# One core, two transformer blocks: the instruction order taken from a simulation of the engines' pipelines

## The chip, the cores and the metric

The kernel runs on one core of a Trainium2 chip. A core has five engines with an instruction queue each: TensorE (PE, with its weight loads as a row of their own, PEld), VectorE (DVE), ScalarE (ACT), GpSimd (POOL) and SyncE (SP), which here only starts DMAs. Each engine works its queue in order; semaphores make it wait for the others. The metric is the device time of one execution in microseconds.

## The reference

Two blocks of two layers each work on 512 positions of 1024 values (the first block puts 16 learned positions ahead: 528), all in float32. Cut to what matters:

```python
# block 1, per layer
proj = rms_norm(h, g) @ w_in                       # q, k, v, xr, gate
q, k = rope(rms_norm(q, gq)), rope(rms_norm(k, gk))        # norms over 64 values of a head
a = softmax(q0 @ k0.T) - lam * softmax(q1 @ k1.T)          # differential attention, causal
o_attn = rms_norm(a @ v, g_sub) * (1 - lam_init)           # norm over 128 values
o_rec = rms_norm(rg_lru(conv(xr)) * gelu(gate), g_rec)
h = h + concat(o_attn, o_rec) @ w_out
g, u = split(rms_norm(h, g2) @ w_gu);  h = h + (silu(g) * u) @ w_down

# block 2, per layer
score = sum_h iw_h * relu(iq_h @ ik.T)             # indexer, 8 heads
keep  = top_k(score, 128)                          # per query
y_dsa = softmax(dq @ dk.T over keep) @ dv          # 6 heads
y_chk = softmax(cq @ ck.T + rel_bias over a band) @ cv     # 6 heads
x = layer_norm(alpha * x + concat(y_conv, y_dsa, y_chk) @ w_out)
x = layer_norm(alpha * x + cross_attention(x, mem))
x = layer_norm(alpha * x + relu(x @ w1) ** 2 @ w2)
```

## The kernel before

Activations lie transposed, features on the 128 partitions and positions along the free dimension. Every weight block (128 columns, 512 KB) comes by a DMA of SP into `wraw`, is rounded by ScalarE to `whi` (L90), and the rest is subtracted by VectorE into `wlo` (L92; 23 blocks on GpSimd). Each product is three matmuls (`mm3`, L96 to L98: high by high, high by low, low by high), so that these three lines make up nearly all of PE's time: 264 columns at a time in block 1, 512 in block 2. `proj` runs the eight `mm3` of a block into a PSUM bank. There are eight banks by name: three `mm` (projections), two `sc` (scores), one each of `tr` (transposes), `av` (row sums and value products) and `bc` (norm factors spread over partitions).

A norm (`rnorm`) goes round four engines: PE sums the squares with the matmuls L166 into `av`; VectorE scales the sum (L170 or L172); `rsqrt` makes the inverse root by a polynomial in twelve small instructions (L136 to L147), which for the norms of queries and keys (`rows`), of the attention's output (`attend1`) and of the recurrent branch (`recout`) run on **GpSimd**: 26 chains in the program. For the 64-wide norms ScalarE then repeats the factors (`nrep`, L179). The transposes L185 spread them into `bc`, and VectorE applies them. The weight products that wait for nothing of this can fill PE's time in between.

Block 1's `attend1` takes a tile of 128 queries: scores into `sc` (L489, the mask L492, L494), their maximum on VectorE (L495), the exponent on ScalarE (L503), the difference of the two softmaxes (L506 to L511), transposes into `tr` (L518, and L523 for the last 16 keys), a split into high and low (L121, L122), and the value product into `av`. The output product `w_out` comes in two halves: the first (`w0`) needs only the recurrent branch (`rh`, `rl`), the second (`w1`) the attention (`bh`, `bl`).

Block 2's mixer first makes the indexer's heads (L898: scores into `sc`; ScalarE's relu L900; VectorE's weighted sum L902), then per block of 128 queries sixteen rounds of VectorE's MAX8 (L913) and MATCH_REPLACE8 (L914), which mark the 128 largest scores. The attention over them (`dsa`) and over the band (`A`) shares `scores` (L851, L852), `attend` (L832 to L839) and `turn` (transposes L845). A layer norm (`Norm.finish`) sums in L730, runs `rsqrt` on VectorE and spreads in L740.

What sets the order: the program is written as a list of steps (STEPS1 for a layer's mixer of block 1, STEPS2 for block 2). The tile framework hands all instructions to a scheduler, which gives each a priority by its place in the program and then simulates the machine: whenever an engine is free in its simulation, it appends to that engine's queue the instruction of the highest priority that is ready there. How long things take in that simulation thus decides what stands ahead of what.

## Time and profile before

| | |
|---|---|
| median of 3 runs | 2938.83 us (2935.24 to 2939.16) |
| the profiled execution | 2940.24 us, span 2938.5 us |
| mean granted TensorE clock | 0.983 |
| PE busy | 2812.4 us, 96% |
| VectorE, ScalarE, GpSimd busy | 58%, 42%, 15% |

The stages of the span, by the lines that run: block 1's first mixer to about 310 us, its feed-forward to 694, the second mixer to 990, its feed-forward to about 1340; block 2's first mixer to about 1610, cross attention, feed-forward; its second mixer from about 2140 to 2410; the last layer norm ends the program. Matmuls are pipelined: the times from start to start tell PE's pace, the durations overlap.

### The profile page before, as it was taken

What the parts mean: (1) busy time and instruction counts of PE and PEld (TensorE: products, weight loads), DVE (VectorE), ACT (ScalarE), POOL (GpSimd) and SP (SyncE); (2) the same over time, 40 slices, a digit from 0 to 9 for tenths busy, and PEclk for the clock granted to TensorE, in tenths of its full rate; (3) what the DMA queues carried; (4) which work ended last, traced back from release to release, by engine and by line L of the source; (5) the groups of instructions that cost most, each with busy time, mean ns of one, the idle gap of its engine ahead of it and who ended that gap; (6) DMA issues with size and microseconds to landing.
All of it is one profiled execution on the core that took longest, in us unless ns stands there. A gap on an engine that the chain in (4) does not pass through costs nothing.

```text
span 2938.5 us, 43082 instructions
## 1 busy us (share of the span) xinstructions
PE 2812.4 (96%) x16556; PEld 2451.3 (83%) x16556; DVE 1700.9 (58%) x3250; ACT 1242.1 (42%) x2218; POOL 446.9 (15%) x715
## 2 busy tenths in 40 slices
PE   7888999999888999999999999999999999999998
PEld 7888999998776788888788888888877898888887
DVE  7666534446766744446997555333589875643335
ACT  5654322224655422223675434322346754333323
POOL 1223000000323000001212021111322120211112
PEclk9999999999999999999999999999999999999999
DMA  4321332322322333334623323333245243223331
GB/s 138 91 70 48 101 94 86 95 87 79 81 72 66 111 94 91 98 91 116 165 74 109 114 65 94 93 97 97 83 113 162 61 129 90 71 94 95 99 94 65
DMA packets 96492, 277.19 MB, mean 94 GB/s; under 512 B 13344, under 2 KB 20000, under 8 KB 96288
## 3 DMA queue, kind: packets, MB, share of 16 engines
q1 hardware_dynamic: 96288, 274.45, 31.7%
q8 instruction: 131, 2.15, 0.3%
q14 instruction: 73, 0.60, 0.1%
HBM read 241.82 MB, written 2.10 MB: 83 GB/s over the span
## 4 chain that ended last, share of the span: by engine, by line
PE 84%; DVE 7%; POOL 3%; issue 2%; ACT 2%; DMA 0%; SPq 0%; ACTq 0%; DVEq 0%; POOLq 0%
PE mm L97 25%; PE mm L98 25%; PE mm L96 25%; PE av L96 1%; DVE wlo L92 1%; PE av L97 1%; POOL nwu L146 1%; PE av L98 1%; PE av L166 1%; PE bc L185 1%; POOL nwu L147 1%; PE bc L845 1%; PE av L730 1%; PE tr L845 1%; PE sc L96 0%
## 5 line engine op out<-in xcount | busy, mean ns | idle before, releaser
L96 PE MATMUL mm<-xh_all,whi 128*128 128x512 f32 (+2 forms) x2752 | 933.5, 341 | 16.4 <-ACT xh_all L269 9.9
L97 PE MATMUL mm<-xl_all,whi 128*128 128x512 f32 (+2 forms) x2752 | 937.6, 341 | 1.2 <-DVE xl_all L270 0.5
L98 PE MATMUL mm<-xh_all,wlo 128*128 128x512 f32 (+2 forms) x2752 | 934.5, 340 | 0.0
L90 ACT CAST whi<-wraw 128x1024 fp32r<-128x1024 f32 (+2 forms) x460 | 465.4, 1013 | 1041.3 <-PE mm L97 857.0
L92 DVE TENSOR_TENSOR wlo<-wraw,whi 128x1024 fp32r<-128x1024 f32 (+2 forms) x437 | 541.1, 1239 | 238.2 <-ACT whi L90 235.7
L96 PEld LDWEIGHTS mm<-xh_all,whi 128*128 128x128 f32 x2752 | 526.5, 192 | 70.5 <-ACT xh_all L269 10.1
L97 PEld LDWEIGHTS mm<-xl_all,whi 128*128 128x128 f32 x2752 | 527.3, 192 | 54.9 <-DVE xl_all L270 1.6
L98 PEld LDWEIGHTS mm<-xh_all,wlo 128*128 128x128 f32 x2752 | 528.4, 192 | 49.9
L1124 POOL TENSOR_TENSOR r<-r 128x512 f32<-128x512 f32 (+1 forms) x70 | 101.8, 1454 | 532.3 <-ACT r L1123 532.3
L98 PE MATMUL mm<-yh,wlo 128*128 128x264 f32 (+1 forms) x528 | 169.4, 321 | 0.0
L96 PE MATMUL mm<-yh,whi 128*128 128x264 f32 (+1 forms) x528 | 169.1, 321 | 0.0
L97 PE MATMUL mm<-yl,whi 128*128 128x264 f32 (+1 forms) x528 | 168.5, 319 | 0.0
L691 DVE TENSOR_TENSOR hall<-hall,mm 128x512 f32<-128x512 f32 (+1 forms) x82 | 46.5, 567 | 144.9 <-PE mm L98 144.9
L611 DVE TENSOR_TENSOR su<-mm,rbc 128x264 f32<-128x264 f32 (+1 forms) x66 | 34.2, 519 | 140.0 <-PE mm L98 140.0
L620 DVE TENSOR_TENSOR hall<-hall,mm 128x264 f32<-128x264 f32 (+1 forms) x72 | 37.1, 515 | 130.7 <-PE mm L98 130.7
L97 PEld LDWEIGHTS mm<-yl,whi 128*128 128x128 f32 x528 | 99.2, 188 | 8.6 <-DVE yl L122 0.6
L98 PEld LDWEIGHTS mm<-yh,wlo 128*128 128x128 f32 x528 | 99.0, 188 | 7.5
L96 PEld LDWEIGHTS mm<-yh,whi 128*128 128x128 f32 x528 | 99.2, 188 | 7.1
L606 DVE TENSOR_TENSOR sg<-mm,rbc 128x264 f32<-128x264 f32 (+1 forms) x66 | 34.0, 517 | 100.4 <-PE mm L98 100.3
L450 POOL MEMSET vh<- 128x128 f32 x8 | 1.6, 204 | 462.0 <-PE mm L98 411.9
L710 POOL TENSOR_TENSOR accq<-accq,nsq 128x512 f32<-128x512 f32 (+1 forms) x48 | 57.6, 1201 | 25.4 <-ACT nsq L708 24.0
L92 POOL TENSOR_TENSOR wlo<-wraw,whi 128x1024 fp32r<-128x1024 f32 x23 | 55.9, 2429 | 36.3 <-ACT whi L90 35.3
(690 smaller groups left out, 5481.7 us busy)
## 6 DMA issues: line engine op xcount, KB each, us to landing
wraw<-w2f SPq DMA_DIRECT2D x128, 512.0 KB, 3.7
wraw<-w1gu SPq DMA_DIRECT2D x88, 512.0 KB, 3.6
wraw<-w2in SPq DMA_DIRECT2D x44, 512.0 KB, 3.9
wraw<-w1in SPq DMA_DIRECT2D x40, 512.0 KB, 3.7
wraw<-w2mkv SPq DMA_DIRECT2D x32, 512.0 KB, 3.7
wraw<-w1dn SPq DMA_DIRECT2D x32, 448.0 KB, 3.3
wraw<-w1out SPq DMA_DIRECT2D x32, 256.0 KB, 2.6
wraw<-w1dn SPq DMA_DIRECT2D x16, 512.0 KB, 3.6
```

The lines of the kernel that those rows point to most:

```text
L90: nc.scalar.copy(hi[:, :kt], raw[:, :kt])
L92: (eng or nc.vector).tensor_sub(lo[:, :kt], raw[:, :kt], f(hi[:, :kt]))
L96: nc.tensor.matmul(ps, wh, xh, start=first, stop=False)
L97: nc.tensor.matmul(ps, wh, xl, start=False, stop=False)
L98: nc.tensor.matmul(ps, wl, xh, start=False, stop=last)
L606: nc.vector.tensor_mul(sg[:, a:b], p, r2[:, a:b])
L611: nc.vector.tensor_mul(su[:, a:b], p, r2[:, a:b])
L620: nc.vector.tensor_add(h[m][:, a:b], h[m][:, a:b], p)
L691: nc.vector.tensor_add(X(m, a, b), X(m, a, b), p)
L710: nc.gpsimd.tensor_add(self.accq[:, a:b], self.accq[:, a:b], sq[:, a:b])
L845: nc.tensor.transpose(ps[:, 128 * j:128 * j + 128], p[:, 128 * j:128 * j + 128], ident)
L1124: nc.gpsimd.tensor_mul(r[:, a:b], r[:, a:b], r[:, a:b])
```

## The change

The scheduler is asked to take its decisions from another simulation, one that follows the engines' pipelines.

```diff
-    with _tile.TileContext(nc) as tc:
+    with _tile.TileContext(nc, schedule_with_timeline_sim=True) as tc:
         both_blocks(tc, *args)
```

The instructions stay the same on every engine, with the same tiles; their order changes on all of them. Three places follow. A name like `mm_657` is one tile: `mm_657`, `mm_736` and `mm_761` are projections, a row with `x6` is six instructions.

PE at the first key's norm in layer 0 of block 1, from the row sums L166 to the transposes L185 that spread the factors, before:

```order
L97 MATMUL mm_657<-xl_all_71,whi_626 128x264
L166 MATMUL av_572<-cs_68,sq_518 88x2 x6
L98 MATMUL mm_657<-xh_all_70,wlo_628 128x264
...
L97 MATMUL mm_736<-xl_all_71,whi_730 128x264
L98 MATMUL mm_736<-xh_all_70,wlo_732 128x264
L185 MATMUL bc_598<-cs_68,nrep_596 128x88 x3
```

and now:

```order
L98 MATMUL sc_482<-xch_471,wgl_231 128x264
L166 MATMUL av_572<-cs_68,sq_518 88x2 x3
L96 MATMUL mm_657<-xh_all_70,whi_626 128x264
...
L98 MATMUL mm_761<-xh_all_70,wlo_732 128x264
L96 MATMUL mm_845<-xh_all_70,whi_839 128x264
L185 MATMUL bc_598<-cs_68,nrep_596 128x88 x3
```

Between the last L166 and L185 stood 28 matmuls of 264 columns; now there are 64, which reach into a third projection.

PE at the end of layer 0's attention (`tr_2960` are the last tile's transposes, `av_2971` its value product, `av_2989` the row sums of its norm, `bc_3013` the spread; `mm_3274` to `mm_3312` are of w_out's first half, `mm_3337` of its second), before:

```order
L98 MATMUL mm_3261<-rh3_2635,wlo_3259 128x264
L518 MATMUL tr_2960<-cs_68,p_2928 128x128 x4
L96 MATMUL mm_3274<-rh0_2567,whi_3257 128x264
...
L96 MATMUL av_2971<-ath_2897,vh_2218 128x256
L96 MATMUL mm_3274<-rh2_2499,whi_3257 128x264
...
L166 MATMUL av_2989<-one2_74,osq_2808 88x2 x6
L98 MATMUL mm_3299<-rh1_2153,wlo_3297 128x264
...
L96 MATMUL mm_3312<-rh3_2635,whi_3295 128x264
L97 MATMUL mm_3312<-rl3_2636,whi_3295 128x264
L185 MATMUL bc_3013<-cs_68,nwy_2998 128x88 x3
```

and now:

```order
L494 MATMUL sc_2947<-k2_2234,qs_1982 128x256
L518 MATMUL tr_2960<-cs_68,p_2928 128x128 x4
L96 MATMUL av_2971<-ath_2897,vh_2218 128x256
L523 MATMUL tr_2967<-cs_68,p_2928 16x128
L97 MATMUL av_2971<-atl_2898,vh_2218 128x256
...
L98 MATMUL av_2971<-ath_2897,vl_2219 128x256
L166 MATMUL av_2989<-one2_74,osq_2808 88x2 x6
L185 MATMUL bc_3013<-cs_68,nwy_2998 128x88 x3
L185 MATMUL bc_3017<-cs_68,nwy_2998 128x88 x3
L96 MATMUL mm_3337<-bh3_3023,whi_3333 128x264
```

All of w_out's first half now stands ahead of the last tile's scores; from L494 to the second half nothing stands between the steps of the chain.

PE in layer 0 of block 2, where the indexer's last heads (`sc_13571` to `sc_13596`) meet the first score pairs (`mm_14031`, `mm_14074` are projections), before:

```order
L898 MATMUL sc_13596<-ik_13086,iq_13085 128x512
L824 MATMUL bc_13774<-cs_68,rt_13745 128x128 x4
L96 MATMUL mm_14031<-xh_all_70,whi_14027 128x512
L851 MATMUL sc_13783<-dkh_13071,dq_13070 128x256
L852 MATMUL sc_13783<-dkl_13072,dq_13070 128x256
L97 MATMUL mm_14031<-xl_all_71,whi_14027 128x512
...
L851 MATMUL sc_13796<-dkh_13071,dq_13070 128x256
L852 MATMUL sc_13796<-dkl_13072,dq_13070 128x256
```

and now:

```order
L98 MATMUL mm_14074<-xh_all_70,wlo_14072 128x512
L898 MATMUL sc_13571<-ik_13086,iq_13085 128x512
L898 MATMUL sc_13576<-ik_13086,iq_13085 128x512
...
L898 MATMUL sc_13596<-ik_13086,iq_13085 128x512
L851 MATMUL sc_13783<-dkh_13071,dq_13070 128x256
L852 MATMUL sc_13783<-dkl_13072,dq_13070 128x256
L851 MATMUL sc_13796<-dkh_13071,dq_13070 128x256
L852 MATMUL sc_13796<-dkl_13072,dq_13070 128x256
...
L845 MATMUL tr_13792<-cs_68,p_13787 128x128
```

Six heads of the indexer and four score pairs now follow each other with no projection in between; the projections of `mm_14031` and `mm_14074` stand ahead of them.

## Rows read from the trace of the kernel before

**Rows 1.** The page: busy time by engine, and the chain that ended last.

```profile
PE 2812.4 (96%) x16556; PEld 2451.3 (83%) x16556; DVE 1700.9 (58%) x3250; ACT 1242.1 (42%) x2218; POOL 446.9 (15%) x715
PE 84%; DVE 7%; POOL 3%; issue 2%; ACT 2%; DMA 0%; SPq 0%; ACTq 0%; DVEq 0%; POOLq 0%
```

**Rows 2.** Windows (stretch, length; PE, PEld, DVE, ACT, POOL busy; clock; DMA): mixers, feed-forward.

```profile
22.00:310.00 288.00, 255.73 (x1952) 240.49 (x1953) 197.24 (x431) 163.31 (x327) 71.89 (x207) 0.94 0.28 78
300.00:375.00 75.00, 74.98 (x621) 74.76 (x621) 38.07 (x66) 24.52 (x31) 0.00 (x0) 1.00 0.32 99
694.00:990.00 296.00, 259.72 (x1563) 222.85 (x1564) 206.49 (x424) 166.10 (x317) 70.50 (x198) 0.94 0.28 77
```

**Rows 3.** Waits of PE (line, releaser: us in total, times, longest).

```profile
PE bc L185 <- ACT nrep L179: 31.5, 15, 3.2
PE bc L185 <- POOL nwy L147: 19.8, 10, 3.0
PE bc L740 <- DVE nwy L154: 10.9, 10, 3.7
...
PE sc L898 <- ACT p L900: 7.3, 9, 1.7
PE tr L518 <- DVE p L511: 5.5, 10, 1.1
```

**Rows 4.** Timeline (start, duration; idle time before and its releaser): first GpSimd chain.

```profile
51.60 1.10 PE L166 MATMUL av<-cs,sq 128*88 128x2 f32 x12
...
55.40 1.30 POOL L147 TENSOR_TENSOR nwu<-nwu,nwt 88x12 f32<-88x12 f32 x1
55.40 1.22 DVE L92 TENSOR_TENSOR wlo<-wraw,whi 128x1024 fp32r<-128x1024 f32 x1 [0.19 <-ACT whi L90]
...
58.33 0.21 POOL L147 TENSOR_TENSOR nwy<-nwu,nwy 88x12 f32<-88x12 f32 x1
58.58 0.83 ACT L179 COPY nrep<-nwy 88x768 f32<-88x768 f32 x1 [3.20 <-POOL nwy L147]
...
59.46 0.51 PE L185 MATMUL bc<-cs,nrep 88*128 88x88 f32 x3 [3.24 <-ACT nrep L179]
```

**Rows 5.** Timeline: the last GpSimd chain, one without L179.

```profile
952.83 0.25 PE L166 MATMUL av<-one,osq 128*128 128x2 f32 x1
...
957.67 0.32 PE L185 MATMUL bc<-cs,nwy 128*128 128x128 f32 x1 [1.84 <-POOL nwy L147]
```

**Rows 6.** Windows: PE at the first chain's end, and the stretch after it.

```profile
59.80:63.00 3.20, 3.20 (x18) 3.20 (x17) 1.61 (x4) 2.65 (x4) 0.10 (x1) 0.50 0.02 5
63.10:66.50 3.40, 3.40 (x30) 3.40 (x29) 3.40 (x4) 0.82 (x1) 1.70 (x1) 1.00 0.00 0
```

**Rows 7.** Timeline: one softmax tile of block 1, scores to transposes.

```profile
261.80 0.36 PE L494 MATMUL sc<-k,qs 128*128 128x256 f32 x1
...
262.20 0.42 DVE L495 TENSOR_REDUCE st<-sc 128x1 f32<-128x256 f32 x1
...
263.38 0.49 ACT L503 ACTIVATE p<-sc,st 128x272 f32<-128x272 f32 x1 [0.32 <-DVE st L501]
...
264.49 0.38 DVE L506 TENSOR_TENSOR st<-st 128x1 f32<-128x1 f32 x1
...
265.41 0.74 ACT L510 ACTIVATE p<-p,st 128x528 f32<-128x528 f32 x1 [1.00 <-DVE st L509]
...
266.18 1.23 DVE L511 SCALAR_TENSOR_TENSOR p<-p,st 128x528 f32<-128x528 f32 x1 [0.17 <-ACT p L510]
...
267.56 0.30 PE L518 MATMUL tr<-cs,p 128*128 128x128 f32 x1 [0.60 <-DVE p L511]
```

**Rows 8.** Windows: the top-k stretch of block 2, both layers.

```profile
1400.00:1510.00 110.00, 105.78 (x542) 84.99 (x543) 108.41 (x310) 73.11 (x165) 23.89 (x36) 1.00 0.50 136
2196.00:2310.00 114.00, 108.78 (x551) 87.12 (x550) 108.70 (x316) 72.94 (x167) 23.08 (x36) 0.99 0.48 132
```

**Rows 9.** Lines of VectorE by form (count; us busy, mean ns; idle before).

```profile
L913 DVE MAX8 m<-isc 128x8 f32<-128x512 f32 x32 | 21.9, 684 | 0.1
```

## The prediction

> **What bounds the kernel now.** I read the page first, then the busy times by stage, the waits of TensorE (PE), and then single chains in the timeline. PE is busy 96% of the span and carries 84% of the chain that ended last [rows 1]. So an order can win only what PE loses by waiting or by a low clock, and can lose what it uncovers. By stage: in the feed-forward stretch PE never waits and issues 621 matmuls of 264 columns in 75.0 us, 0.121 us each [rows 2]; no order helps there. In block 1's two mixer stretches PE is busy 255.7 of 288 us and 259.7 of 296 us, at a mean granted clock of 0.94 [rows 2]: that is where time lies. The waits say what ended PE's idle time [rows 3]: most is at L185, the transposes that spread a norm's result, 31.5 us behind ScalarE's copy L179 and 19.8 us behind GpSimd's last step L147. Everything else is small: 10.9 us for the LayerNorm's L740, 7.3 us for the indexer's L898, 5.5 us for the softmax's L518.
>
> **The change part by part.** No instruction is added or removed; each engine still runs its list in order, and only the lists differ. So I counted, for each chain that leaves PE and comes back, the PE work that stands between the two ends (its cover) at the paces of rows, and set it against the chain's time in the trace. Where the cover is shorter, PE waits for the difference.
>
> *A, the GpSimd norm chains.* The first one starts at 51.60 and its L185 starts at 59.46; L166 itself takes 1.1 us, so the chain proper is 6.7 us [rows 4]. Before, 28 matmuls stand in between (28 x 0.121 = 3.4 us) and PE waits 3.24 us [rows 4]; the new order puts 64 there, 7.7 us, and the wait is gone. The last chain runs from 952.83 to 957.67 with a wait of 1.84 us [rows 5]. There are 26 such chains (16 with L179, 4.7 to 7.3 us; 10 without, 3.75 to 4.9 us), 139 us in all. Their covers sum to 71 us before and 159 us now. Chain by chain the shortfall is 68 us before, of which rows 3 show 31.5 + 19.8 = 51 us, and 21 us after: eight chains stay short, two of them with nothing in between. I take the ratio on the measured wait plus the issue gap around it: 63 x (68 - 21) / 68 = 43, so **-42** (-36 if only the 51 us shrink, -47 if all the 68 do).
>
> What the chain's length rests on shows in its fifth GpSimd pair: L147 takes 1.30 us where the same operation takes 0.21 us later, and it starts at the instant at which DVE starts the 1.22 us subtraction L92 [rows 4]. The Trainium skill, page "SBUF — State Buffer", section "Who interferes with whom", says that a DVE instruction with two SBUF inputs contends with a GpSimd instruction that reads SBUF, that one fully blocks the other, and that the order of issue decides which; the trace agrees, 1.30 against 0.21 us. By that rule the new DVE order could lengthen the chains: an estimate with each at the length of the longest seen gives a shortfall of 32 in place of 21 us, 11 us more in the sum; I don't count it.
>
> *B, the clock in block 1.* After such a wait the clock falls: in the 3.2 us from 59.80 PE issues 18 matmuls at a granted clock of 0.50 (1.2 of 2.4 GHz), in the 3.4 us after that 30 at 1.00 [rows 6]. 5.6 against 8.8 per us: each us at half speed costs 0.36 us. A mean of 0.94 over 288 and 296 us [rows 2] is about 35 us at half speed in each, 12 to 13 us lost in each, 25 in all. Fewer long waits, fewer falls; but C makes new ones. Half: **-12** (0 to -25).
>
> *C, the softmax at phase ends.* In the middle of the phases nothing is lost. But the new order spends the projections and output weights early, and at the end of a phase none is left between a tile's last score L494 and its transposes L518. In six tiles the cover falls from 3.9 to 5.6 us to 0.3, 1.8, 0, 3.0, 2.0 and 0 us (7.1 in all). A tile's own operations add up to 0.36 + 0.42 + 0.49 + 0.38 + 0.74 + 1.23 = 3.6 us, and with the queues between them it took 267.56 - 261.80 = 5.8 us [rows 7]. So 6 x 3.6 - 7.1 = 14.5 at best and 6 x 5.8 - 7.1 = 28 at worst; **+17**, near the bare end, because the weight splits in those queues have then been done. What follows such a tile is bare too: the split of the transposed block before the value product (four times), the second transpose (five), the first output matmul (three). Twelve steps at about 0.7 us (the nearest row is ScalarE's copy of 0.83 us [rows 4]): **+8** (0 to 10). The query's DMAs stand nearer to their first score: **+4** (0 to 10). Block 1 thus gives -25.
>
> *D, the top-k stretch of block 2.* Here DVE, not PE, is full: busy 108.4 of 110 us and 108.7 of 114 us [rows 8], with 32 of the largest MAX8 at 0.684 us [rows 9] and as many replacements. PE loses little there (105.8 of 110 busy), because projections stand among the scores. The new order groups the scores and pulls the projections ahead, so PE reaches consumers of DVE earlier. Over the same 50 us of PE work, 83 us of DVE work (each instruction at its row's mean) stand ahead of what PE needs next, before 68. Counted from the first rope on, DVE falls behind by 18.6 us where it was 7.3 in the first layer, and by 18.1 where it was 5.6 in the second: +11 to +12 per layer, **+23** (0 if the top-k steps give way, +34 if the largest lag, 17 each, counts in full).
>
> *E, the rest of block 2's scores.* They stand in rows of eight on two banks; today L898 waits 7.3 us in nine pieces [rows 3], 0.8 us each. Ten more such waits: **+8** (0 to 30). *F, the closing LayerNorms*: covers go up in one half and down in the other; chains of 7 to 12 us against 5 to 18 us of cover give **+4** (-2 to 12) against today's 10.9 us [rows 3]. *G, the clock in block 2*: if D's and E's 31 us of waits bring half-speed stretches as in rows 6, some 22 us of them at 0.36: **+8** (0 to 14). The start, the feed-forward stages and the end of the program keep their order within a few matmuls and cost nothing: PE work covers them as now.
>
> Sum: -42 - 12 + 17 + 8 + 4 + 23 + 8 + 4 + 8 = +18 on the profiled execution's 2940.24 us, 2958. That run lies 1.4 us above the median of the three (2938.83), so **2957**. All low ends give -60, all high ends +102.
>
> **The rivals.** *Faster.* The chain gain stays and the DVE of the top-k stretch keeps up, because a top-k step only has to be done when its block's mask is used, and its lag (18 us) may be smaller than the PE work queued at that place. Place: the score pairs L851 and L852 of block 2. It decides from the point at which DVE's lag stays under what PE still has ahead; then D, E and G vanish: -42 - 12 + 17 + 8 + 4 + 4 = -21, and -34 with the whole of the clock's 25: 2905 to 2918, middle 2912. For it speaks that DVE is busy only 58% of the span [rows 1] and that the total DVE work is the same; against it that in that stretch it has nothing to spare [rows 8]. *No change*: the order doesn't bring what it is built for; the waits that A takes away come back as C, D and the same number of clock falls (A -42, B 0, C and its train +29, D +13): 2939. *Far slower*: the grouped chains queue as before's do (5.8 us for 3.6, up to 14 us for a tile in the middle of a phase). By those times the shortfall over every chain of the program would be 306 us where it was 153; the high ends of C to G are then the better prices: about +70, 3010.
>
> **How the numbers follow.** My forecast, a net loss of 6 to 50 us, has 0.45; faster 0.30; no change 0.15; far slower 0.10. The time is the first case's, 2957; its own range is 2945 to 2990. The range runs from the faster rival's low end to below the far slower one: 2905 to 3000, leaving out 0.1 on each side. A measurement of this kernel tells some 0.2% (6 us) from no change, so: faster 0.30, same 0.15, slower 0.55.
>
> **What would show it.** In the new profile: PE's wait at L185 behind L179 and L147 down from 51 to about 15 to 20 us (A); the mean clock of the mixer stretches at 0.96 to 0.97 (B); PE's wait at L518 up from 5.5 to over 20 us, at the end of each layer's attention (C); in the top-k stretch PE waiting for DVE or for ScalarE behind it by 10 us or more per layer, DVE still full (D). The forecast is wrong if that stretch takes its 110 us as before, or if the softmax tiles at the phase ends start their transposes without a wait.

## The result: 4.3% slower, outside the range

The changed kernel takes **3063.9 us** (median of 4 runs, 3061.13 to 3071.68) against 2938.99 us: a ratio of 1.0432, interval 1.0412 to 1.0453. Slower was the forecast's side, but 18 us were forecast and 125 came; even the "far slower" rival stood at 3010.

The page after, the lines that answer to [rows 1] (busy time by engine; the chain that ended last):

```profile
PE 2866.4 (94%) x16556; PEld 2502.1 (82%) x16556; DVE 1689.1 (55%) x3250; ACT 1244.8 (41%) x2222; POOL 449.9 (15%) x715
PE 77%; DVE 11%; ACT 4%; DMA 3%; issue 2%; POOL 1%; SPq 1%; DVEq 0%; ACTq 0%; POOLq 0%
```

The span went from 2938.5 to 3059.3 us, by 120.8. PE runs the same 16556 matmuls, but is busy 54.0 us longer (2866.4 against 2812.4): they ran slower. The other 66.8 us are idle time. The mean granted clock fell from 0.983 to 0.960; the stretches at half clock add up to 249 us in the trace after and 102 us before, and (249 - 102) x 0.36 = 53 us, an estimate with the price of a half-speed us that the prediction took from [rows 6], is as much as the longer busy time. So the loss has **two parts: 67 us of waits and 54 us of longer busy time, by this estimate nearly all of it the clock**. Stage by stage the estimate doesn't come out: in the table below the longer busy time (length less idle) is 7 us for 38 us at half clock in each of block 1's mixers, but 19 for 34 and 13 for 17 in block 2's. Part of block 2's is something else: the records count a matmul with nothing behind it for its whole duration, in place of the time to the next start, and PE stands idle 137 times in block 2 where it was 52.

Where it lies, by the starts of the last matmul of each stage (length; how much longer after; of it PE idle; half-clock time more), in us:

| stage | before | after | idle | at half clock |
|---|---|---|---|---|
| block 1, mixer of layer 0 (to the end of w_out) | 303.4 | +13.9 | +6.6 | +38 |
| block 1, mixer of layer 1 | 284.4 | +11.1 | +3.8 | +38 |
| block 2, mixer of layer 0, with the norm ahead | 245.7 | +38.6 | +19.5 | +34 |
| block 2, mixer of layer 1, with the norm ahead | 258.3 | +35.1 | +21.8 | +17 |
| the other nine stages together | 1846.7 | +22.1 | +15.1 | +20 |

What PE waits for after, beside [rows 3] (line, releaser: us in total, times, longest):

```profile
PE tr L518 <- DVE p L511: 17.7, 4, 6.0
PE sc L851 <- DVE st L832: 15.1, 25, 1.7
PE av L166 <- ACT sq L415: 14.7, 4, 5.1
PE mm L96 <- DVE hall L691: 10.2, 6, 2.9
...
PE bc L740 <- DVE nwy L154: 8.5, 5, 4.1
PE sc L898 <- ACT p L900: 8.5, 7, 2.6
PE bc L185 <- POOL nwy L147: 7.7, 2, 3.9
PE av L166 <- ACT osq L532: 6.2, 6, 1.8
...
PE bc L185 <- ACT nrep L179: 4.6, 4, 2.2
```

The GpSimd norms did what term A said: 31.5 + 19.8 us at L185 became 4.6 + 7.7. The softmax at phase ends did what term C said: L518 went from 5.5 to 17.7. New or grown are the row sums L166, 14.7 us behind ScalarE's squares L415 of the *next* query or key norm, and 6.2 behind L532, the squares of the attention's output; L96 behind L691 (none before), a projection that waits until VectorE has added an earlier one out of its bank; and L851, in 25 small pieces. The two of them that stood in the list before:

```profile
PE av L166 <- ACT sq L415: 3.2, 4, 1.1
PE sc L851 <- DVE st L832: 1.9, 2, 1.0
```

The stretches that answer to [rows 2] and [rows 8] (stretch, length; PE, PEld, DVE, ACT, POOL busy; clock; DMA):

```profile
22.00:317.00 295.00, 255.64 (x1897) 242.32 (x1896) 189.71 (x402) 162.42 (x326) 76.72 (x208) 0.88 0.26 72
707.00:1004.00 297.00, 255.17 (x1515) 224.19 (x1514) 193.55 (x402) 164.91 (x313) 75.15 (x203) 0.88 0.26 71
1430.00:1560.00 130.00, 112.31 (x502) 87.90 (x501) 106.32 (x301) 67.78 (x155) 22.27 (x36) 0.88 0.41 110
2270.00:2400.00 130.00, 112.05 (x510) 87.24 (x509) 105.40 (x301) 67.97 (x154) 22.52 (x35) 0.92 0.42 110
```

Block 1's mixers fell from a clock of 0.94 to 0.88, the top-k stretch from 1.00 and 0.99 to 0.88 and 0.92. And VectorE, full in that stretch before (108.4 of 110), has room after (106.3 of 130).

### The profile page after: what moved, and what is told of

Its sections match the earlier page's. It is cut to its first block, busy times and chain, and to the rows that moved or that the text cites. A ratio compares the mean times of both kernels' runs of the same rounds, so it can differ in the third digit from the quotient of the medians.

```text
span 3059.3 us, 43072 instructions
## 1 busy us (share of the span) xinstructions
PE 2866.4 (94%) x16556; PEld 2502.1 (82%) x16556; DVE 1689.1 (55%) x3250; ACT 1244.8 (41%) x2222; POOL 449.9 (15%) x715
## 4 chain that ended last, share of the span: by engine, by line
PE 77%; DVE 11%; ACT 4%; DMA 3%; issue 2%; POOL 1%; SPq 1%; DVEq 0%; ACTq 0%; POOLq 0%
PE mm L96 23%; PE mm L97 23%; PE mm L98 23%; DVE wlo L92 1%; PE av L97 1%; PE av L96 1%; PE av L98 1%; SPq L863 1%; DVE isc L914 1%; ACT whi L90 1%; PE av L166 1%; DMA dq<-nl 1%; DVE m L913 1%; DVE hall L720 1%; DVE p L832 1%
## 5 line engine op out<-in xcount | busy, mean ns | idle before, releaser
L96 PE MATMUL mm<-xh_all,whi 128*128 128x512 f32 (+2 forms) x2752 | 938.9, 343 | 18.2 <-ACT xh_all L269 9.9
L92 DVE TENSOR_TENSOR wlo<-wraw,whi 128x1024 fp32r<-128x1024 f32 (+2 forms) x437 | 536.2, 1228 | 250.0 <-ACT whi L90 247.4
L96 PEld LDWEIGHTS mm<-xh_all,whi 128*128 128x128 f32 x2752 | 532.0, 194 | 79.1 <-ACT xh_all L269 10.1
L97 PEld LDWEIGHTS mm<-xl_all,whi 128*128 128x128 f32 x2752 | 533.6, 194 | 62.7 <-DVE xl_all L763 5.4
L98 PEld LDWEIGHTS mm<-xh_all,wlo 128*128 128x128 f32 x2752 | 534.6, 194 | 56.1 <-DVE wlo L92 2.3
L96 PE MATMUL mm<-yh,whi 128*128 128x264 f32 (+1 forms) x528 | 168.6, 321 | 0.0
L691 DVE TENSOR_TENSOR hall<-hall,mm 128x512 f32<-128x512 f32 (+1 forms) x82 | 45.5, 567 | 153.6 <-PE mm L98 153.6
L96 PEld LDWEIGHTS mm<-yh,whi 128*128 128x128 f32 x528 | 99.0, 188 | 6.9
L92 POOL TENSOR_TENSOR wlo<-wraw,whi 128x1024 fp32r<-128x1024 f32 x23 | 55.7, 2423 | 88.7 <-ACT whi L90 88.6
L503 ACT ACTIVATE p<-sc,st 128x272 f32<-128x272 f32 (+4 forms) x88 | 45.6, 521 | 43.8 <-DVE st L495 23.5
```

The costliest lines, as they stand in the source:

```text
L92: (eng or nc.vector).tensor_sub(lo[:, :kt], raw[:, :kt], f(hi[:, :kt]))
L96: nc.tensor.matmul(ps, wh, xh, start=first, stop=False)
L97: nc.tensor.matmul(ps, wh, xl, start=False, stop=False)
L98: nc.tensor.matmul(ps, wl, xh, start=False, stop=last)
L503: nc.scalar.activation(p[:n, a:b], ps[:n, :b - a], AF.Exp, bias=mx, accum_out=st[:n, o + 3 + e:o + 4 + e])
L691: nc.vector.tensor_add(X(m, a, b), X(m, a, b), p)
```

## The experiments

The instructions of both kernels are the same under the same names, so an order can be carried from one program to the other: the program is first scheduled both ways, the queues of each engine are noted (`old`, `new`), and in a third pass dependencies without a wait hold an engine to a noted queue. What is not held, the scheduler of that run decides, in the same pass and so with the held queue before it. The code cuts of this section are shortened to the idea.

```diff
+    for queue in rule(traced):               # the queues that this kernel holds
+        for a, b in zip(queue, queue[1:]):
+            tc.add_manual_dep(by[b], a, no_sync, reason="order")
```

### Which half of the program, which engine's queue

`first_new`: `rule` gives block 1's part of all queues from `new`, block 2's from `old`; `second_new` the other way round.

> All engines take the new order in block 1 and the old one in block 2. In the trace after, block 1 ends 33 us later than before (1344.1 to 1377.5 us at the last down-projection). If the stages lose independently: 2939 + 33 = 2972 us, with the clock of both mixer stretches at 0.88. If block 1's loss were given back or made larger by what block 2's order expects of it: under 2955 or over 2990.

> The old order in block 1, the new one in block 2. Independent stages: 2939 + (121 - 33) = 3027 us, of it some 38 us in each mixer. If block 2 only suffers from what block 1 hands over: under 2990.

Measured: **2972.5** (ratio 1.0114, 1.0099 to 1.0129) and **3032.0** (1.0317, 1.0302 to 1.0333). 33 + 93 us, against 125 for both: the two halves lose independently, near the sizes of the stage table (33 and 87).

`pe_old`: the new scheduler, `rule` returns `[old["PE"]]`. `pe_new`: the old one with `[new["PE"]]`. `dve_old`: the new one with `[old["DVE"]]`.

> The scheduler decides by the pipelines' simulation, but TensorE's own order is held to that of the kernel before; the other engines' queues are free and come out of the new simulation. Theory 1 (TensorE's order is the cause: work that could fill is spent early and the chains stand bare): the loss goes, 2930 to 2960 us. Rival (the other engines' orders are the cause: on VectorE and ScalarE other work stands ahead of what TensorE waits for): 3020 us or more.

> The other half: the scheduler of before, TensorE held to the new order. Theory 1: 3030 to 3070 us. Rival: 2940 to 2970 us, since the other queues are again made by the old simulation.

> The new scheduler with VectorE's queue held to the old order; the other four queues are free. If VectorE's order is the cause: 2980 us or less. If an order only fits as a set with the others made with it (theory 2, after the two runs that held TensorE's queue): 3050 us or more, as those.

Measured: **3061.3**, **3158.2** and **3299.7** us. My theory 1 fell: with the old TensorE queue the new scheduler is as slow as with its own. But the rival is not shown either, for with the new TensorE queue the old scheduler is slower still, above both expectations. In `pe_old` PE waits for the GpSimd norms again and for more besides (its lines stand 3 further down):

```profile
PE bc L188 <- ACT nrep L182: 33.2, 13, 5.2
PE bc L188 <- POOL nwy L150: 27.0, 10, 3.9
PE bc L743 <- DVE nwy L157: 23.1, 7, 4.0
PE sc L901 <- ACT p L903: 11.4, 11, 2.2
```

These are other waits than the new order's, at other stages: block 1's mixers are 23.0 and 17.4 us longer than before, block 2's only 18.2 and 16.4. So neither TensorE's nor VectorE's queue alone carries the loss. Each hold of one queue, with the others made round it by the scheduler that did not make that queue, costs 120 to 360 us, while all queues held together (`first_new`, `second_new`) cost what the stage table says. This speaks for orders that fit as a set; a hold of one queue under its own scheduler, which would show what the hold itself costs, was not run.

### Is the new simulation worse, or were the step lists fitted to the old one?

`plain_old` and `plain_new`: STEPS1 and STEPS2 in plain order (all `r`, then key, query, value and attention head by head, gates last; block 2 likewise, with its top-k steps in the order of their blocks), old and new scheduler.

> The old scheduler with the step lists in plain order: in block 1 all recurrent parts first, then head by head key, query, value, attention, and the gates at the end; in block 2 projections, indexer, then dsa, then the bands. It is the base for the next kernel; 20 to 150 us over 2939, since less matrix work is left to lie beside the chains.

> The new scheduler with the same plain lists. Theory 3 (the lists of the kernel are fitted to the orders that the old scheduler makes of them, the new simulation as such is no worse): within 40 us of the plain lists with the old scheduler, on either side. Theory 4 (the new simulation makes worse orders of any list): 80 us or more over it.

Measured: **3176.8** and **3260.5** us. The base is 238 us over the kernel before, more than the 150 expected. With lists that nobody fitted, the new scheduler is 84 us slower, against 125 with the kernel's own: theory 4, at its edge. So the fit of the lists is not needed for the new simulation to lose; how much of the 125 is the fit one other list can't settle.

### Terms A and B alone

`covered`: the old scheduler, TensorE's old queue, in which 24 of the 26 spreads L185 are moved back past other matrix work.

```diff
+    for sums, spread in CHAINS:              # L166s and L185s of a GpSimd norm
+        later(spread, 7.5, q.index(sums[-1]))    # us of matrix work in between
+    return [q]
```

> Terms A and B alone: the old scheduler and TensorE's old order, in which only the spreads L185 of 24 of the 26 GpSimd norms are moved back, past other matrix work, until about 7.5 us of it stand ahead of them (where enough is there); the two norms of the recurrent branch stay. If the forecast's sizes for A and B hold: the wait at L185 behind L179 and L147 falls from 51 to under 20 us, the clock of block 1's mixers rises, 2880 to 2905 us. Rival (what is moved ahead is missing later, and the softmax tiles or the following norms stand bare, as in the new order): 2930 us or more.

Measured: **3002.3** us (1.0216, 1.0200 to 1.0233). The rival: the following norms do stand, though not for want of cover. PE's waits there (its lines stand 5 to 11 further down; L172 is the row sums, L426 the squares, L194 the spread, L428 the product that empties `bc`):

```profile
PE av L172 <- ACT sq L426: 44.4, 10, 5.8
PE sc L500 <- ACT p L514: 13.7, 11, 2.6
PE bc L194 <- DVE raw L428: 12.4, 8, 4.1
PE bc L194 <- POOL nwy L152: 11.2, 7, 3.5
```

Of the norms' waits 11.2 us are left of 51, and 44.4 us came back at the next norm's row sums (3.2 before), 13.7 at the scores L500. Why, the trace after shows at its longest L166 wait (timeline; start, duration):

```profile
162.50 0.45 PE L185 MATMUL bc<-cs,nrep 88*128 88x88 f32 x3 [0.82 <-DVE raw L417]
163.64 0.48 DVE L417 SCALAR_TENSOR_TENSOR raw<-raw,par,bc 128x264 f32<-128x264 f32 x1
166.03 0.71 DVE L420 TENSOR_TENSOR sq<-sq,ct 128x528 f32<-128x528 f32 x1
168.03 0.69 DVE L421 TENSOR_TENSOR raw<-raw,sq 128x528 f32<-128x528 f32 x1
168.75 0.63 ACT L121 CAST nh<-raw 128x528 fp32r<-128x528 f32 x1 [1.58 <-DVE raw L421]
169.29 0.64 ACT L415 ACTIVATE sq<-raw 128x528 f32<-128x528 f32 x1
169.98 0.31 PE L166 MATMUL av<-cs,sq 128*88 128x2 f32 x1 [5.11 <-ACT sq L415]
```

The tile `sq` has one buffer and two lives in `rows`: it holds the squares (L415), and after the norm the rotated half of the rope (L418 to L421). The next norm's squares need it back. So a spread that comes later makes the next L166 later. The trace alone doesn't prove it: ScalarE's queue has the key's split L121, which waits for L421 too, ahead of the squares. `apart_old`, `covered_apart` and `apart_new` give the squares another buffer, which stands in the layer anyway:

```diff
+    ss = small.tile([128, T], F32, name="ss_sq", bufs=2)
-    nc.scalar.activation(sq[:, a0:b0], raw[:, a0:b0], AF.Square)
+    nc.scalar.activation(ss[:, a0:b0], raw[:, a0:b0], AF.Square)
```

> The old scheduler and the old lists; in the norms of queries and keys the squares go to a buffer of their own (one of two that stand in the layer already), so that the next norm's squares need not wait until the rope has let go of the buffer. In the old order nothing waits there: 2930 to 2950 us. Base for the next kernel.

> The kernel with the spreads L185 moved back, whose TensorE waited 44 us for the squares L415 in place of the norms, with the squares in a buffer of their own as in the run before. If that one buffer is what gave the gain of terms A and B back: the wait at L166 for L415 falls under 10 us, 2900 to 2930 us. Rival (the next thing in line, the softmax tiles and the score banks behind the later keys, takes it): 2960 us or more.

> The new scheduler with the squares of the query and key norms in a buffer of their own (under the old one that changed nothing, 2939 us). If the one buffer, for which TensorE waits 14.7 us at L166 in the trace after, is a cause of block 1's loss: block 1 is 15 us or more shorter with the clock it gives back, 3035 to 3050 us. Rival (it is only the wait that ends last there): 3055 us or more.

Measured: `apart_old` **2939.2** us (0.9998, 0.9989 to 1.0008): nothing under the old order, as expected. `covered_apart` **2954.6**, between its two expectations: 48 us of `covered`'s loss of 64 are gone and L166's wait is 8.3 us, but it is still not faster than before. Its longest wait is now at the one bank `bc`, whose second half waits 15.0 us until VectorE has emptied the first; whether that is what keeps it from gaining was not tested. `apart_new` **3028.7** us, 35 us faster than the change as made and below the range expected. Its first mixer beside the window of block 1 above, and its wait at the softmax's transposes (two lines further down there):

```profile
22.00:300.00 278.00, 250.04 (x1925) 237.74 (x1925) 191.03 (x408) 160.38 (x325) 84.01 (x208) 0.90 0.28 78
```

```profile
PE tr L520 <- DVE p L513: 4.3, 2, 4.1
```

By stages block 1's mixers are now 6.8 and 8.6 us *shorter* than before, where they were 13.9 and 11.1 longer. But the new scheduler made other orders with that buffer: the wait at the transposes fell too, from 17.7 to 4.3 us, with no change to what the softmax works on. So the buffer, and the order that the scheduler makes with it, turned block 1's loss into a gain; what the buffer brings with the order of the change kept was not run.

`mix1_new` draws the conclusion: the squares apart, `rule` gives the new scheduler's order for this kernel in block 1's two mixers alone, the old everywhere else.

> The new order in block 1's two mixers alone, with the squares in a buffer of their own, where it made them 7 and 9 us shorter than the old; the old order everywhere else. If terms A and B hold as soon as that buffer is out of the way, and the stages are independent: 2939 - 16 = 2923 us, the lowest of all. Rival (the gain is given back at the stage's end, where the old order takes over): 2935 us or more.

Measured: **2924.2** us (0.9945, 0.9933 to 0.9958), the forecast of its expectation to 1 us, and **faster than both kernels**. The window that answers to the first of [rows 2]:

```profile
22.00:310.00 288.00, 262.17 (x2032) 249.88 (x2031) 198.49 (x425) 165.44 (x332) 84.39 (x208) 0.92 0.29 80
```

The clock there is 0.92, *lower* than the 0.94 before. Over the whole program PE stands idle 10 us less than before (115.9 against 126.0 us), and yet the half-clock time is 133 us where it was 102. Of the gain between the profiled executions 10 us are waits; the other 5 are shorter busy time in spite of the lower clock, and no run here says why.

### The clock

`warm`: every queue in the old order; ahead of each GpSimd norm's spread 14 matmuls whose result the spread overwrites.

```diff
+    if eng is nc.gpsimd and j0 == 0:
+        for _ in range(14):
+            nc.tensor.matmul(ps[:, :264], xh_all[:, 0, :128], xh_all[:, 0, :264], start=True, stop=True)
```

> The kernel before, every queue in the old order, with 14 matmuls of 264 columns that nobody needs (14 x 0.121 = 1.7 us, into the bank that the spread overwrites) straight ahead of the spread L185 of each GpSimd norm, where TensorE waits 1.1 to 3.4 us now. If the clock of block 1's mixers falls because TensorE stands idle there: 72 us at half clock become 25 or less, and 0.36 x 47 = 17 us are won, minus some 5 us where the wait was shorter: 2920 to 2932 us. Rival (the clock follows something else): the half-clock time stays, 2938 to 2948 us.

Measured: **2932.8** us (0.9975, 0.9965 to 0.9985), just at the upper end of the range expected (2932). 364 matmuls more, and less time. The page's line on busy time, and the window over block 1's first mixer:

```profile
PE 2834.9 (97%) x16920; PEld 2475.1 (85%) x16920; DVE 1701.7 (58%) x3250; ACT 1241.4 (42%) x2218; POOL 445.5 (15%) x715
```

```profile
22.00:300.00 278.00, 263.58 (x2094) 248.69 (x2095) 193.93 (x422) 162.91 (x327) 72.07 (x207) 0.98 0.27 78
```

Block 1's mixers run at 0.98 in place of 0.94 and are 5.6 and 4.3 us shorter; the half-clock time of the program is 48 us where it was 102. 364 x 0.121 = 44 us of work were added. PE's idle time fell by 32 us (from 126 to 94), so 12 us of that work had no wait to fill; its busy time grew by 22.5 us only, so 21 to 22 us were won by the clock, which 54 x 0.36 = 19 bears out: 10 us net between the profiled executions, as the stages show, and 7 between the medians. So in block 1's mixers of the old order it is the standing idle at these spreads that lowers the clock. The sum of idle time is no measure of it, as `mix1_new` shows.

### Block 2

`two_rounds_old`, `two_rounds_new`: `if r % 8 == 0:` ahead of MAX8 and MATCH_REPLACE8.

> The old scheduler, with 2 of the 16 rounds of MAX8 and MATCH_REPLACE8 left, so that VectorE has over 80 us less to do in each of block 2's mixers: it leaves out most of the top-k. Base for the next kernel: TensorE already loses only 10 and 13 us in these mixers, so at most 20 us less than 2939.

> The same with the new scheduler; most of the top-k is left out here too. Term D (VectorE full of top-k rounds is what TensorE waits for): the two mixers of block 2, which are 38.6 and 35.1 us longer under the new order, are now at most 12 us longer each than with the old one, and the whole is some 70 us over the kernel with two rounds and the old order. Rival (score banks, grouped scores and the orders of the other engines, with top-k or without): 30 us longer each, 110 us or more in all.

Measured: **2948.6** and **3052.1** us, 103 us apart; the first is 10 us slower than with all rounds, where at most 20 less had been expected. The mixers of block 2 are 36.0 - 5.4 = 30.6 and 31.1 + 0.6 = 31.7 us longer than with the old scheduler, with most of the top-k gone; 38.6 and 35.1 with all of it: the rounds account for 8 and 3 us. Term D's mechanism is there, as the wait at the score pairs shows, 6.7 us where it was 15.1 (4.7 with the old scheduler), but it is not what makes these mixers longer in the main:

```profile
PE sc L851 <- DVE st L832: 6.7, 18, 1.1
```

`bank_old`, `bank_new`: three score banks, two for projections.

```diff
-    BANKS = {"mm": 3, "sc": 2, "tr": 1, "av": 1, "bc": 1}
+    BANKS = {"mm": 2, "sc": 3, "tr": 1, "av": 1, "bc": 1}
```

> The old scheduler with three banks for scores and two for projections (three and two the other way round before). Base for the next kernel; a projection's bank is read out while the next one runs, so two nearly do: 2930 to 2970 us.

> The new scheduler with three banks for scores, two for projections. If the grouped scores on two banks are what makes block 2's mixers long (term E, the wait at L851 of 25 us in both layers): that wait falls under 8 us, the mixers come to within 20 us of those of the run before each, and the whole to within 85 us. Rival: still 30 us each and 110 us or more in all.

Measured: **2987.3** (above its range) and **3094.3** us. The difference, 107 us, and the mixers' (23.0 and 29.6 us, where 38.6 and 35.1 were) lie between the two theories. The wait that should have gone did not, but the two banks for projections brought a longer one of their own at L691, so what a third score bank would do by itself is not settled:

```profile
PE mm L96 <- DVE hall L691: 24.4, 7, 4.4
PE sc L851 <- DVE st L832: 20.2, 28, 2.7
```

`natural_new`: `apart_new`, with the projections' high and low parts in three pairs of buffers by turns (`n`, and `da` and `ca` while the attention does not use them).

> The new scheduler, the squares apart as in the run before, and in block 2 the projections that go to their heads by DMA (indexer, dsa's queries, the band's keys) are split into buffers of their own by turns (those of the attention's transposed weights, which are not in use yet) where one pair served all. In the trace after, VectorE and ScalarE wait for these DMAs to let go of that pair (dq<-nl is the longest piece of the chain there), and TensorE behind them. If that is what makes block 2's mixers long: each is 15 us or more shorter than in the run before (3028.7), 2985 to 3005 us. Rival (the orders as such, spread over many small waits at the score banks): less than 8 us each, 3012 us or more.

Measured: **3022.8** us, 6 less than `apart_new`; the mixers are 2.0 and 3.6 us shorter. The rival. What makes block 2's mixers longer **stays open**: it is for the most part neither the top-k rounds nor that pair of buffers, and a third score bank in place of one for projections does not remove it. In `pe_old` they are about half as much longer, but with other waits, so that this doesn't tell the queues' shares.

## Why the prediction was wrong

*A held.* The first chain's spread now starts 8 us after its row sums, and PE no longer waits for it:

```profile
53.62 0.56 PE L166 MATMUL av<-cs,sq 128*88 128x2 f32 x6
60.28 0.83 ACT L179 COPY nrep<-nwy 88x768 f32<-88x768 f32 x1 [1.75 <-POOL nwy L147]
61.93 0.39 PE L185 MATMUL bc<-cs,nrep 88*128 88x88 f32 x3
```

The waits at L185 fell by 39 us, forecast -42. *C held*: L518's wait rose by 12.2 us behind L511, and by 4.0 behind L501 (17 forecast), and the last tile of layer 0, with nothing between its scores and its transposes, cost what its row says:

```profile
275.73 0.36 PE L494 MATMUL sc<-k,qs 128*128 128x256 f32 x1
279.32 0.77 DVE L511 SCALAR_TENSOR_TENSOR p<-p,st 128x528 f32<-128x528 f32 x1 [0.86 <-ACT p L510]
280.23 1.09 PE L518 MATMUL tr<-cs,p 128*128 128x128 f32 x4 [4.14 <-DVE p L511]
```

280.23 - 275.73 = 4.5 us for the tile: between the 3.6 and 5.8 that bounded it, nearer the lower, as taken.

*The step that failed first is that A's time was taken as won.* I asked for each moved spread what stood behind it on TensorE, and not **who waits for a buffer that its chain holds**. The prediction's own counting of chains began at L166; that L166 itself stands at the end of a chain that begins with the previous norm's spread was not in it. A and C were to give 13 us less idle time in block 1's mixers, and 10 more came (6.6 + 3.8): a miss of 23. Of it 11.5 us are L166 behind the squares L415 (14.7 against 3.2), and 6.2 are L166 behind L532, which the prediction's list of bare steps at the phase ends lacks. `covered` and `covered_apart` show the first at its plainest: 44.4 us of waits, and 48 us of time with the buffer apart.

*The second, and the largest, is the clock (B and G).* Forecast: -12 and +8 us. Measured: 54 us of longer busy time, with 147 us more at half clock. The term was counted from the long waits alone, as if the falls of the clock went with them. But waits moved elsewhere lower it as well, and so do shorter ones. Even where A's waits are gone and the squares have their buffer, the clock of block 1's first mixer is 0.92 and not the 0.96 to 0.97 that the prediction gave as its sign (`mix1_new`). In block 2, the clock fell for 17 us, from 1456.9 on, where PE had been busy 14.0 of 17 us; the longest wait up to there is the one of 1.78 us in which the fall begins (windows, then timeline):

```profile
1440.00:1457.00 17.00, 14.03 (x61) 10.69 (x60) 16.45 (x40) 7.09 (x13) 4.93 (x3) 1.00 0.24 71
1457.00:1474.00 17.00, 10.90 (x26) 7.23 (x27) 15.50 (x47) 8.42 (x21) 0.14 (x1) 0.50 0.58 140
1474.00:1490.00 16.00, 16.00 (x77) 13.29 (x76) 15.38 (x45) 7.24 (x20) 4.82 (x2) 1.00 0.26 66
```

```profile
1455.01 0.98 PE L898 MATMUL sc<-ik,iq 128*128 128x512 f32 x2 [0.93 <-ACT p L900]
1457.78 0.80 PE L898 MATMUL sc<-ik,iq 128*128 128x512 f32 x1 [1.78 <-ACT p L900]
```

No fixed price of a wait comes out of the runs: over the whole program 54 us came with 67 us of waits, but by the table 10 us more idle time brought 75 us at half clock in block 1's mixers, and 41 brought 51 in block 2's; in `mix1_new` 10 less brought 31 more. Which waits lower the clock, by their length or their places, stays open.

*D was mis-sized, and block 2's mixers lost what no term held.* VectorE full for 110 us looked like a limit; it was mostly work that could wait: the rounds account for 11 us where D gave 23. *E* looked at the wrong place: L898's wait rose by 1.2 us, L851's by 13.2 (8 forecast). D, E and G were to give 39 us there and 74 came: 41 of waits, and 32 of longer busy time, where G had 8 for the clock. *F* held: the closing norms' waits at L740 rose by about 2 us (4 forecast). But the prediction put the other nine stages at nothing beside F, and they lost 22 us. In block 1's feed-forward stages (2.7 and 5.8 us) PE now waits for the norm at their start, at L185; in block 2, for L691 and in many small pieces.

By stages the forecast's miss of 103 us is then 50 in block 1's mixers (-25 forecast, +25 measured), 35 in block 2's, 18 in the rest. The rival "faster" had no case here; but part of its gain, 15 us, can be had in block 1 (`mix1_new`). The reading of [rows 3] that "everything else is small" left out 9.9 us at L96 behind L269, which came back the same after and changed nothing. The rule of the Trainium skill weighed in term A ("SBUF — State Buffer", "Who interferes with whom") shows again after: in the first chain an L147 takes 1.12 us beside an L92 of 1.23 us; A's gain came within 3 us of its forecast all the same.

## What to carry to other kernels

When an order covers a chain with more work, follow the buffers of that chain to their next user before booking the gain: a tile with one buffer and two lives makes the next chain start where this one ends. Count what the clock may cost beside the waits, for short waits as for long, and don't take fewer waits for a higher clock: read the half-clock time of a run, for it followed no sum of waits here. A wait that can't be covered can be filled with work that nobody needs (7 us won here). Holding one engine's queue and letting the scheduler make the others cost 120 to 360 us here, while whole stages, with all their queues, can be taken from either order: block 1's mixers from the new one, with the buffer apart, and all else from the old beat both kernels.

## What was not expected of the hardware

364 useless matmuls (44 us of work) made the kernel 7 us faster, since the clock held at 0.98 instead of 0.94 in block 1's mixers, where they filled waits of up to 3.2 us. An order with 10 us less idle time ran at a lower clock (0.92 for 0.94 in the first mixer). And the clock fell to half for 17 us after a stretch in which PE was busy 14.0 of 17 us and no wait was longer than 1.8 us.
